# Gates as one stacked fp32r product, and a norm's factors made a row by two fp32r products, in a two-layer decoder trunk

## The chip, the cores and the metric

The kernel runs on 1 core of one Trainium2 chip. The metric is the device time of one execution in microseconds (us). The engines are PE (matrix products; PEld is its loading of weights), DVE (vector), ACT (scalar, activation functions), POOL and SP (here it issues the transfers). L12 is line 12 of the kernel before.

## The reference

The input is 256 tokens of width 2048, with 256 memory tokens. Layer 0 mixes with gated linear attention (GLA, 4 heads), layer 1 with forgetting attention; both cross-attend into the memory, and each is followed by a gated MLP of width 5632 with a short convolution. Everything is fp32. What the change touches is the norm, used throughout, and the gates of GLA:

```python
def rmsnorm(x, g):
    xf = x.astype(jnp.float32)
    y = xf * lax.rsqrt(jnp.mean(xf * xf, axis=-1, keepdims=True) + EPS)
    return (y * g.astype(jnp.float32)).astype(x.dtype)
...
    z = h @ w_in
    q, k, v, glr, og, mq = split_cols(
        z, [GLA_QK_WIDTH, GLA_QK_WIDTH, GLA_V_WIDTH, GLA_GATE_RANK, GLA_V_WIDTH, MEM_WIDTH])
    g = jax.nn.log_sigmoid((glr @ w_gate_up + b_gate).astype(jnp.float32)) / GLA_GATE_TAU
```

`glr` has 16 columns, `w_gate_up` is 16 x 1024.

## The kernel before, in words

**Products.** A PE product takes fp32 operands, or fp32r ones, which hold fewer bits. The large projections keep fp32 accuracy by three fp32r products: each weight tile `raw` (loaded by SP, L189) is rounded to `whi` by ACT (L190), and the rest, `wlo = raw - whi`, comes from DVE (L199). Activations are split in the same way (`split`, L283) into the pairs in `bufA` and `bufB`. The product of the two rests is left out. `raw` has four buffers, `whi` and `wlo` three each.

**Two kinds of projection.** `proj_fm` (L202) gives outputs with features on the partitions: for each of 16 row blocks and two column blocks, L224 multiplies `whi` by both parts side by side (512 columns) and L225 `wlo` by the high part (256 columns); L227 closes. `proj_tm` (L237) gives outputs with tokens on the partitions (L261, L262, L263). Together they are nearly all of PE's work.

**Norms.** The factor of a norm is one number per token, and it is applied to a projection's result. `Norm.col` (L328) makes it as a column, tokens on the partitions, by a sum and three Newton steps on DVE (L323 to L326). `Norm.row` (L339) makes of it a row that is the same on all partitions: DVE builds a diagonal matrix of the factors, `dg`, by two products of the identity with a column (L345), PE multiplies a matrix of ones by it in fp32 (L347), and ACT copies the result (L350). This happens nine times: for the memory's norm, for the mixer's norm of layer 0, for each of four GLA heads, for the two MLP norms, and for the norm that keys, values and layer 1's mixer share. `dg` takes a buffer of the tag "sq", of which there are two, and which the squares of the norms use too (L302, L363).

**Gates.** The first value projection of GLA has the 16 gate columns beside it. `turned` (L267) takes them: ACT writes them, scaled, into `narrow`, a tile of zeros (L273), PE transposes it (L278), and ACT copies the result to `glr` (L490): 16 used rows of 128. For each head, `gates` (L505) loads its 128x256 weights `wg` (L509; two buffers; rows beyond 16 are zeros) and makes two fp32 products of 128x256 (L513), whose results go through Abs, Exp and Ln on ACT (L516 to L518) and a scan on DVE (L522). `turned` serves the forget gates of layer 1 as well (L658).

**Order.** A scheduler orders the instructions of each engine when the program is built, from the dependences, from estimated times, and from a priority that draws the weight loads and splits ahead (`tc.high_priority`, L194). Engines then run their lists in order. SP's list holds nearly all loads.

Of the kernel before, what the change touches and what calls it, by code (L numbers as in the profile page):

```python
# [12 lines left out]
F32 = mybir.dt.float32  # L13
F32R = mybir.dt.float32r
I32 = mybir.dt.int32
AF = mybir.ActivationFunctionType
ALU = mybir.AluOpType
PSUM = bass.MemoryType.PSUM

P = 128  # L20
T = 256
# [4 lines left out]
GLA_H, DK, DV = 4, 256, 384  # L26
FOX_H, HD = 12, 128
MEM_H = 4
RANK = 16
# [107 lines left out]
def _trunk(ctx: ExitStack, tc: tile.TileContext, xt, xtok, memt, wp, wgu, gns, gfin, cnv, par, msk, out):  # L137
    nc = tc.nc
    where, _ = _layout()
    V, S, TE = nc.vector, nc.scalar, nc.tensor  # L140

    const = ctx.enter_context(tc.tile_pool(name="const", bufs=1))
    wpool = ctx.enter_context(tc.tile_pool(name="wpool", bufs=4))
    sm = ctx.enter_context(tc.tile_pool(name="small", bufs=2))
# [9 lines left out]
    ident = mask[:, M_ID : M_ID + P]  # L154
    ones = mask[:, M_ONE : M_ONE + P]
# [3 lines left out]
    def gain(name, i):  # L159
        c = C_GAIN[name] + i  # L160
        return gains[:, c : c + 1]

    eps = const.tile([P, 1], F32, name="eps")
    nc.gpsimd.memset(eps, EPS)

# [10 lines left out]
    def work(tag, bufs=1):  # L176
        return pwork.tile([P, 512], F32, name="ps_" + tag, tag=tag, bufs=bufs)
# [86 lines left out]
                if u == len(units) - 1:  # L264
                    evac(b, a)

    def turned(pool, bank, width, col):  # L267

        t = pool.tile([P, T], F32, name="narrow", tag="tmp", bufs=5)
        nc.gpsimd.memset(t, 0.0)  # L270

        def take(b, a):
            S.activation(t[:, b * P : b * P + width], a, AF.Copy, scale=col[:, b : b + 1])  # L273

        def turn():
            for b in range(2):
                bs = slice(b * P, (b + 1) * P)
                TE.transpose(bank[:, bs], t[:, bs], ident)  # L278
            return bank[:, :T]

        return take, turn
# [11 lines left out]
    class Norm:  # L293
# [45 lines left out]
        def row(self):  # L339

            if self.r is None:
                y = self.col()
                dg = sm.tile([P, T], F32, name="dg", tag="sq", bufs=2)
                for b in range(2):
                    V.tensor_scalar(dg[:, b * P : (b + 1) * P], ident, y[:, b : b + 1], None, ALU.mult)  # L345
                pr = work("t")
                TE.matmul(pr[:, :T], ones, dg, start=True, stop=True)  # L347
                self.r = sm.tile([P, T], F32, name="row", tag="rowx" if self.tag == "x" else "row",
                                 bufs=2 if self.tag == "x" else 1)
                S.activation(self.r, pr[:, :T], AF.Copy)  # L350
            return self.r
# [51 lines left out]
    nx = StreamNorm()  # L403
# [65 lines left out]
    def gla(nx):  # L469
        h, mix = bufB, bufA  # L470
        with tc.tile_pool(name="gla", bufs=1) as gp:
# [3 lines left out]
                nc.gpsimd.memset(t, 0.0)  # L475
            on = {}

            glr = gp.tile([P, T], F32, name="glr")

            def values(hd):  # L480
                return gp.tile([P, 2, DV], F32, name="gv", tag="gv", bufs=2)

            v0 = values(0)
            take, turn = turned(gp, work("t"), RANK, nx.col())

            def first_values(b, a):
                S.activation(v0[:, b, :], a[:, :DV], AF.Copy, scale=nx.col()[:, b : b + 1])
# [17 lines left out]
            def gates(hd):  # L505

                bc = gp.tile([P, 2, T], F32, name="bc", tag="bc", bufs=2)
                wg = gp.tile([P, DK], F32, name="wg", tag="wg", bufs=2)
                nc.sync.dma_start(wg, wgu[hd])  # L509
                for c in range(2):  # L510
                    f = 2 * hd + c
                    ps = work("s", 2)
                    TE.matmul(ps[:, :T], wg[:, c * P : (c + 1) * P], glr, start=True, stop=True)  # L513
                    bias = part[:, C_BG + f : C_BG + f + 1]
                    e = gp.tile([P, T], F32, name="ge", tag="tmp", bufs=5)
                    S.activation(e, ps[:, :T], AF.Abs, bias=bias)  # L516
                    S.activation(e, e, AF.Exp, scale=-1.0)
                    S.activation(e, e, AF.Ln, bias=1.0)  # L518
                    mz = gp.tile([P, T], F32, name="gm", tag="tmp", bufs=5)
                    V.tensor_scalar(mz, ps[:, :T], bias, 0.0, ALU.add, ALU.min)  # L520
                    V.tensor_tensor(mz, mz, e, ALU.subtract)
                    V.tensor_tensor_scan(bc[:, c, :], scanmask, mz, 0.0, ALU.mult, ALU.add)  # L522
                return bc
# [100 lines left out]
            for hd in range(GLA_H):  # L624
                bc = gates(hd)
                q = gp.tile([P, 2, T], F32, name="gq", tag="gq", bufs=2)
                k = gp.tile([P, 2, T], F32, name="gk", tag="gk", bufs=2)
                v = values(hd) if hd else v0
                proj_fm(("gq", hd), h, lambda c, a: V.scalar_tensor_tensor(
                    q[:, c, :], whole(a), DK ** -0.5, nx.row(), ALU.mult, ALU.mult))  # L630
                proj_fm(("gk", hd), h, lambda c, a: V.tensor_tensor(k[:, c, :], whole(a), nx.row(), ALU.mult))
                if hd == GLA_H - 1:
                    for j in range(OG_EARLY):
                        take_og(j)
                if hd:
                    proj_tm(("gv", hd), h, lambda b, a: S.activation(
                        v[:, b, :], a, AF.Copy, scale=nx.col()[:, b : b + 1]))
                core(hd, q, k, v, bc)
# [4 lines left out]
    def fox(nx, vt):  # L643
        hk, hq, mix = bufB, bufA, bufB
        stash = vt.rearrange("p b (i t) -> p (b i) t", t=T)
        with (
# [9 lines left out]
            cs = fp.tile([P, T], F32, name="fc")  # L656
            cc = fp.tile([P, 2, FOX_H], F32, name="fcc")
            take, turn = turned(fp, work("s", 2), FOX_H, nx.col())  # L658

            def forget():  # L660
# [120 lines left out]
    def preparing(name, dst, also=None):  # L781
# [18 lines left out]
        return n, then  # L800

    gla(nx)
    n, then = preparing("ffn0", bufB)
    add_out(("wo", 0), bufA, then)
# [18 lines left out]
    with tc.tile_pool(name="store", bufs=1) as op:  # L823
        gf = op.tile([P, D], F32, name="gf")
        nc.sync.dma_start(gf, gfin.to_broadcast([P, D]))
        y = op.tile([P, 2, 512], F32, name="y")
# [93 lines left out]
```

## Time and profile before

| | |
|---|---|
| median of 3 runs | 2309.28 us (2309.21 to 2309.69) |
| the profiled execution: its own time | 2308.97 us |
| its span, first to last instruction | 2307.2 us |
| granted PE clock | 0.999 |
| busy PE, DVE, ACT | 2289.1, 1605.6, 1251.5 us |
| weight splits L199 (DVE) | 972.6 us in 809 |
| weight roundings L190 (ACT) | 843.2 us in 809 |
| PE records of L347 (row) and L513 (gates) | 18 and 16 |
| mean transfer rate | 186 GB/s |

Each group of the profile names the line, the engine, the operation, the tiles (out<-in) and the shapes, then the busy time, the mean duration of one, and the engine's idle time just before, with what ended it. Durations of PE records overlap, since products follow each other in its pipe; what a product costs is read from the distance between starts. A product of fp32 operands leaves two records of products and two of weight loads, one of fp32r operands a single one of each.

### The profile page before, as it was taken

What the parts mean: (1) busy time and instruction counts of PE and PEld (TensorE: products, weight loads), DVE (VectorE), ACT (ScalarE), POOL (GpSimd) and SP (SyncE); (2) the same over time, 40 slices, a digit from 0 to 9 for tenths busy, and PEclk for the clock granted to TensorE, in tenths of its full rate; (3) what the DMA queues carried; (4) which work ended last, traced back from release to release, by engine and by line L of the source; (5) the groups of instructions that cost most, each with busy time, mean ns of one, the idle gap of its engine ahead of it and who ended that gap; (6) DMA issues with size and microseconds to landing.
All of it is one profiled execution on the core that took longest, in us unless ns stands there. A gap on an engine that the chain in (4) does not pass through costs nothing.

```text
span 2307.2 us, 32826 instructions
## 1 busy us (share of the span) xinstructions
PE 2289.1 (99%) x12256; PEld 1986.0 (86%) x12256; DVE 1605.6 (70%) x2595; ACT 1251.5 (54%) x1954; POOL 3.0 (0%) x19
## 2 busy tenths in 40 slices
PE   8999999999999999999999999999999999999998
PEld 7889998888888888888888998888888888888886
DVE  7567877577774777557767557657776577756775
ACT  6555555455553555445565455556554455534554
POOL 0000000000000000000000000000000000000000
PEclk9999999999999999999999999999999999999999
DMA  8655455655555555655555564565556555565554
GB/s 305 204 161 158 147 163 166 192 185 185 190 192 191 192 186 189 192 192 191 187 186 184 172 207 151 163 198 183 191 186 192 194 187 191 186 196 190 186 191 155
DMA packets 124744, 430.27 MB, mean 186 GB/s; under 512 B 14108, under 2 KB 18600, under 8 KB 124456
## 3 DMA queue, kind: packets, MB, share of 16 engines
q1 hardware_dynamic: 124296, 427.65, 57.6%
q8 instruction: 96, 1.57, 0.3%
q10 hardware_dynamic: 288, 0.52, 0.1%
q14 instruction: 64, 0.52, 0.1%
HBM read 426.01 MB, written 2.11 MB: 186 GB/s over the span
## 4 chain that ended last, share of the span: by engine, by line
PE 98%; DMA 0%; ACT 0%; DVE 0%; issue 0%; SPq 0%; DVEq 0%; ACTq 0%
PE acc L224 37%; PE acc L225 20%; PE acc L262 12%; PE acc L263 12%; PE acc L261 12%; PE acc L227 2%; PE ps_s L588 1%; PE ps_s L794 0%; PE ps_t L379 0%; PE ps_s L386 0%; PE ps_o L397 0%; DMA mt<-memt 0%; PE ps_s L708 0%; PE ps_o L602 0%; PE ps_o L724 0%; PE ps_s L557 0%
## 5 line engine op out<-in xcount | busy, mean ns | idle before, releaser
L199 DVE TENSOR_TENSOR wlo<-raw,whi 128x1024 fp32r<-128x1024 f32 (+4 forms) x809 | 972.6, 1203 | 554.1 <-ACT whi L190 541.4
L190 ACT ACTIVATE whi<-raw 128x1024 fp32r<-128x1024 f32 (+4 forms) x809 | 843.2, 1043 | 779.6 <-PE acc L263 366.6
L224 PE MATMUL acc<-B,whi 128*128 128x512 f32 x1980 | 683.4, 395 | 0.0
L224 PE MATMUL acc<-A,whi 128*128 128x512 f32 x1680 | 580.6, 396 | 7.4 <-ACT whi L190 7.4
L225 PE MATMUL acc<-B,wlo 128*128 128x256 f32 x2112 | 551.4, 281 | 0.0
L225 PE MATMUL acc<-A,wlo 128*128 128x256 f32 x1792 | 464.5, 281 | 0.5 <-DVE wlo L199 0.5
L224 PEld LDWEIGHTS acc<-B,whi 128*128 128x128 f32 x1980 | 361.0, 188 | 68.3
L225 PEld LDWEIGHTS acc<-B,wlo 128*128 128x128 f32 x2112 | 397.6, 188 | 20.8
L224 PEld LDWEIGHTS acc<-A,whi 128*128 128x128 f32 x1680 | 305.8, 188 | 64.0 <-ACT whi L190 7.7
L225 PEld LDWEIGHTS acc<-A,wlo 128*128 128x128 f32 x1792 | 338.1, 189 | 21.0 <-DVE wlo L199 1.2
L262 PE MATMUL acc<-wlo,B 128*128 128x512 f32 (+3 forms) x736 | 275.4, 374 | 1.2 <-DVE wlo L199 1.2
L263 PE MATMUL acc<-whi,B 128*128 128x512 f32 (+3 forms) x736 | 273.7, 372 | 0.0
L261 PE MATMUL acc<-whi,B 128*128 128x512 f32 (+3 forms) x736 | 247.8, 372 | 0.0
L262 PE MATMUL acc<-wlo,A 128*128 128x512 f32 x544 | 212.4, 390 | 0.0
L263 PE MATMUL acc<-whi,A 128*128 128x512 f32 x544 | 212.0, 390 | 0.0
L261 PE MATMUL acc<-whi,A 128*128 128x512 f32 x544 | 192.8, 391 | 0.0
L232 ACT ACTIVATE part<-acc 128x256 f32<-128x256 f32 x240 | 90.1, 375 | 165.4 <-PE acc L227 165.4
L262 PEld LDWEIGHTS acc<-wlo,B 128*128 128x128 f32 x736 | 138.2, 188 | 20.6 <-DVE wlo L199 1.5
L263 PEld LDWEIGHTS acc<-whi,B 128*128 128x128 f32 x736 | 138.2, 188 | 18.9
L261 PEld LDWEIGHTS acc<-whi,B 128*128 128x128 f32 x736 | 137.4, 188 | 18.7
L234 DVE TENSOR_TENSOR wholes<-acc,part 128x256 f32<-128x256 f32 x240 | 101.0, 421 | 67.4 <-ACT part L232 67.3
L263 PEld LDWEIGHTS acc<-whi,A 128*128 128x128 f32 x544 | 102.1, 188 | 21.2
(196 smaller groups left out, 1576.1 us busy)
## 6 DMA issues: line engine op xcount, KB each, us to landing
raw<-wp SPq DMA_DIRECT2D x743, 512.0 KB, 3.4
raw<-wp SPq DMA_DIRECT2D x32, 384.0 KB, 3.1
raw<-wp SPq DMA_DIRECT2D x24, 388.0 KB, 3.1
raw<-wp SPq DMA_DIRECT2D x8, 400.0 KB, 3.1
xf<-xt SPq DMA_DIRECT2D x16, 128.0 KB, 4.7
x<-xtok SPq DMA_DIRECT2D x4, 512.0 KB, 7.1
mt<-memt SPq DMA_DIRECT2D x3, 512.0 KB, 7.8
cb<-cdram SPq DMA_DIRECT2D x12, 128.0 KB, 3.4
```

The lines of the kernel that those rows point to most:

```text
L190: casts.append(S.activation(hi[:, s], raw[:, s], AF.Copy))
L199: V.tensor_tensor(lo[:, s], raw[:, s], hi[:, s].bitcast(F32), ALU.subtract)
L224: TE.matmul(a, hi[:, s], both, start=done == 0, stop=False)
L225: TE.matmul(a[:, :T], lo[:, s], both[:, 0, :], start=False, stop=False)
L227: TE.matmul(a, hi[:, s], both, start=False, stop=True)
L232: S.activation(t, a[:, T:], AF.Copy)
L234: V.tensor_tensor(r, a[:, :T], t, ALU.add)
L261: TE.matmul(a, xk[:, 0, xs], hi[:, s], start=u == 0 and j == 0, stop=False)
L262: TE.matmul(a, xk[:, 0, xs], lo[:, s], start=False, stop=False)
L263: TE.matmul(a, xk[:, 1, xs], hi[:, s], start=False, stop=last)
L588: TE.matmul(ps[:, b * NVER : (b + 1) * NVER], kt[:, c, b * P : (b + 1) * P], dd[:, 2 * c + b, :], start=c == 0, stop=c == 1)
```

## The change

Both fp32 products named above become fp32r products.

The row: the factors `y` are split into a rounded part and the rest, each a column pair in fp32r. For each part DVE makes a diagonal tile of 128x256 by one product of the identity with the broadcast column, and PE multiplies a tile of ones in fp32r (filled once by POOL) by it; the two products add up in one accumulator.

The gates: the three partial products of a split multiplication (high by high, high by rest, rest by high) are laid along the rows that were zeros. `narrow` now holds the rounded gate columns at 0 and at 32 and their rest at 64; the weights hold the same 16 rows three times, and rows 32 to 63 are replaced by the rest of the rounding, so that one fp32r product sums all three. `wg` is loaded as `raw`, rounded by ACT and its middle rows are subtracted by DVE; `wgraw` and `wg` have one buffer each. The forget gates of layer 1 keep the old way.

```diff
+    onesr = const.tile([P, P], F32R, name="onesr")
+    nc.gpsimd.memset(onesr.bitcast(F32), 1.0)
...
-    def turned(pool, bank, width, col):
+    def turned(pool, bank, width, col, parts=False):
...
         def take(b, a):
-            S.activation(t[:, b * P : b * P + width], a, AF.Copy, scale=col[:, b : b + 1])
+            o = [t[:, b * P + i : b * P + i + width] for i in (0, 32, 64)]
+            if not parts:
+                S.activation(o[0], a, AF.Copy, scale=col[:, b : b + 1])
+                return
+            for i in range(2):
+                S.activation(o[i].bitcast(F32R), a, AF.Copy, scale=col[:, b : b + 1])
+            V.scalar_tensor_tensor(o[2], a, col[:, b : b + 1], o[0], ALU.mult, ALU.subtract)
...
                 y = self.col()
-                dg = sm.tile([P, T], F32, name="dg", tag="sq", bufs=2)
-                for b in range(2):
-                    V.tensor_scalar(dg[:, b * P : (b + 1) * P], ident, y[:, b : b + 1], None, ALU.mult)
+                y2 = [sm.tile([P, 2, 1], F32R, name=f"y{i}", tag=f"y{i}") for i in range(2)]
+                V.tensor_copy(y2[0], y.unsqueeze(2))
+                V.tensor_tensor(y2[1], y.unsqueeze(2), y2[0].bitcast(F32), ALU.subtract)
                 pr = work("t")
-                TE.matmul(pr[:, :T], ones, dg, start=True, stop=True)
+                for i, yi in enumerate(y2):
+                    dg = sm.tile([P, 2, P], F32R, name="dg", tag="sq", bufs=2)
+                    V.tensor_tensor(dg, ident.unsqueeze(1).to_broadcast([P, 2, P]),
+                                    yi.bitcast(F32).to_broadcast([P, 2, P]), ALU.mult)
+                    TE.matmul(pr[:, :T], onesr, dg, start=i == 0, stop=i == 1)
...
-            glr = gp.tile([P, T], F32, name="glr")
+            glr = gp.tile([P, T], F32R, name="glr")
...
-            take, turn = turned(gp, work("t"), RANK, nx.col())
+            take, turn = turned(gp, work("t"), RANK, nx.col(), True)
...
-                wg = gp.tile([P, DK], F32, name="wg", tag="wg", bufs=2)
-                nc.sync.dma_start(wg, wgu[hd])
+                raw = gp.tile([P, DK], F32, name="wgraw", tag="wgraw")
+                nc.sync.dma_start(raw, wgu[hd])
+                wg = gp.tile([P, DK], F32R, name="wg", tag="wg")
+                S.activation(wg, raw, AF.Copy)
+                V.tensor_tensor(wg[32:64], raw[32:64], wg[32:64].bitcast(F32), ALU.subtract)
...
-    wgu[:RANK] = a["gla_w_gate_up"][0]
+    for i in (0, 32, 64):
+        wgu[i : i + RANK] = a["gla_w_gate_up"][0]
```

## The prediction

> **What bounds the kernel now.** I read the page first: the busy shares, then the chain that ended last.
>
> ```profile
> PE 2289.1 (99%) x12256; PEld 1986.0 (86%) x12256; DVE 1605.6 (70%) x2595; ACT 1251.5 (54%) x1954; POOL 3.0 (0%) x19
> ...
> PE 98%; DMA 0%; ACT 0%; DVE 0%; issue 0%; SPq 0%; DVEq 0%; ACTq 0%
> ```
>
> The matrix engine (PE) is busy for 99% of the span, and 98% of the last chain is its own products, one after the other. A busy share alone could hide gaps between products, so the view of waits comes next, for PE alone (who waits for whom: us in total, times, longest):
>
> ```profile
> PE acc L224 <- ACT whi L190: 7.4, 1, 7.4
> PE acc L262 <- DVE wlo L199: 1.2, 1, 1.2
> PE acc L225 <- DVE wlo L199: 0.5, 1, 0.5
> ```
>
> PE waits three times: for the first data, once at the start, and once at 1321 us. Nothing else stops it. The granted clock is 0.999. So the kernel lasts as long as its list of products, and a shorter product shortens it one for one, as long as no wait appears.
>
> **What the change takes from PE.** The groups by form show the two products that are replaced, and an fp32r product of the same 256 columns (the last pair of numbers before the bar's idle: busy us, mean ns):
>
> ```profile
> L225 PE MATMUL acc<-B,wlo 128*128 128x256 f32 x2112 | 551.4, 281 | 0.0
> ...
> L347 PE MATMUL ps_t<-dg,mask 128*128 128x256 f32 x18 | 5.3, 378 | 0.0
> L513 PE MATMUL ps_s<-glr,wg 128*128 128x256 f32 x16 | 4.8, 379 | 0.0
> ```
>
> L347 is the norm's row and L513 the gates. An fp32 product leaves two records, so 18 and 16 records are nine rows and eight gate products. The mean durations are no price: products overlap in the pipe, so I take the distance between starts. The timeline of PE around the row of the last GLA head:
>
> ```profile
> 396.56 0.39 PE L261 MATMUL acc<-whi,A 128*128 128x512 f32 x1
> 396.79 0.40 PE L262 MATMUL acc<-wlo,A 128*128 128x512 f32 x1
> 397.02 0.59 PE L347 MATMUL ps_t<-dg,mask 128*128 128x256 f32 x2
> 397.27 0.58 PE L263 MATMUL acc<-whi,A 128*128 128x512 f32 x1
> 397.68 0.63 PE L261 MATMUL acc<-whi,A 128*128 128x512 f32 x2
> ```
>
> From L262 (396.79) to L261 (397.68) are 0.89 us. The same stretch without a row, L262 and L263, takes two steps of 0.23 us (396.56 to 396.79 is one). The row costs 0.89 - 0.46 = 0.43 us. A gate, in the timeline at head 0:
>
> ```profile
> 160.12 0.28 PE L225 MATMUL acc<-B,wlo 128*128 128x256 f32 x1
> ...
> 160.23 0.59 PE L513 MATMUL ps_s<-glr,wg 128*128 128x256 f32 x2
> ...
> 160.47 0.58 PE L224 MATMUL acc<-B,whi 128*128 128x512 f32 x1
> ...
> 160.89 1.02 PE L397 MATMUL ps_o<-pts,mv 128*128 128x256 f32 x4
> ```
>
> From L225 to L397 are 0.77 us, and L225 plus L224 take 0.35 (0.117 + 0.232, the median distances of starts behind these lines in the trace): the gate costs 0.42 to 0.43. So 17 products x 0.43 = **7.31 us** go.
>
> **What it adds on PE.** Nine rows become 18 fp32r products of 128x256, eight gates become eight: 26. In the trace an L225 is followed by an L224 after 117 ns (median of 3,140), and by another L225 after 114 (median of 499). I take 117: 26 x 0.117 = **3.04 us**. The bounds: 0.112 (the lowest tenth) and 0.124 (the highest), so 2.9 to 3.2. Nothing gives a gain below that, since 256 columns are streamed in every case.
>
> One rule of the Trainium skill speaks against this step. Its page "TensorE: Matmul & The Clock Gate", section "The mechanism" of the part on packing, says that a weight load overlaps a running product only when the two use different row groups; here all use the whole array. The same page puts a load of 128 columns at about 107 ns, so 26 loads in the open would be an estimated 2.8 us, and the sum would nearly vanish. The trace disagrees: 499 pairs of L225, each with its own full load (188 ns in the PEld rows), follow at 114 ns, which leaves no room for a load in the open.
>
> **What it adds elsewhere.** Per row, DVE's two diagonal halves become a copy, a difference, and two products of 128x256. The nearest rows:
>
> ```profile
> L572 DVE TENSOR_TENSOR gdd<-bc 128x256 f32<-128x256 f32 x12 | 5.0, 418 | 0.0
> ...
> L345 DVE TENSOR_SCALAR dg<-mask,ny 128x128 f32<-128x128 f32 x18 | 4.3, 283 | 0.2
> L324 DVE TENSOR_TENSOR nt<-nt,nv 128x2 f32<-128x2 f32 x27 | 4.3, 158 | 0.6
> ```
>
> Two L345 take 0.48 us from start to end. The new chain takes two small steps of 0.2 us (L323 to L326 start that far apart) and 2 x 0.42: about 1.24, 0.76 more per row, 6.8 us in nine. The bounds of one wide step are 0.28 (L345, half as wide) and 0.55 (L572 at 384 columns). For the gates come four DVE differences of 32x256 (at most 0.42 each, 1.7 us), four ACT conversions of 128x256 (0.38 by the row's copy at L350, 1.5 us), two more narrow ACT evictions (0.26 by L273 at 12 columns) and two narrow DVE ones (0.16 to 0.35). That is about 9 us of DVE and 2 us of ACT. What hides them: ACT's weight conversions L190 sit idle for 366.6 and 217.0 us until PE (L263, L224) frees a buffer, and DVE's L199 waits 541.4 us for ACT. Both run as far ahead as their three buffers let them. Without that cover each microsecond counts in full, but only inside the buffer's depth, some 2.8 us of PE work per weight tile.
>
> The added waits: PE waits for two diagonals instead of one. How early was the one? At the first channel mixer's row:
>
> ```profile
> 494.53 0.48 DVE L345 TENSOR_SCALAR dg<-mask,ny 128x128 f32<-128x128 f32 x2
> 495.25 1.23 DVE L199 TENSOR_TENSOR wlo<-raw,whi 128x1024 fp32r<-128x1024 f32 x1 [0.24 <-ACT whi L190]
> ...
> 498.83 0.59 PE L347 MATMUL ps_t<-dg,mask 128*128 128x256 f32 x2
> ```
>
> The diagonal is done at 495.01, 3.8 us before PE comes to it; over the nine rows the least is 3.4 us (the head at 327.01). As built, the changed program puts one weight split L199 between the factors' split and the diagonals here and in two more rows, and between the diagonals of two heads. Here: 494.93 after the two small steps, L199 to 496.5, diagonals to 497.3. The built program also sets the products later, some 1.7 us of PE work here, so about 3 us stay. Behind a PE product that waits stand all weight products; behind a DVE diagonal stands the next L199, which PE needs units later. Both diagonals now hold the two "sq" buffers, so ACT's squares wait for the second product; no square is due within several us, except at the memory norm, where they wait for x (landing near 55.9) anyway.
>
> The loads of `wg` stay four of 128 KB (4.2 us to landing), through one buffer. The second now stands behind three more weight loads on SP and waits for the first one's DVE split. SP's weight loads behind it wait for DVE's splits too, and gates are first needed at 160 us, the first load goes out at 39. I put this at nothing. The ones tile is a POOL memset near 0.7 us, against PE's first product at 7.37.
>
> The order moves much else within GLA, but the costly change of shape there, the 64-column products L552, comes in seven runs before and after. The stall at 1321 us follows the forget gates (two ACT table loads, a transfer out and three back on SP); none of it is touched.
>
> **Sum.** 7.31 - 3.04 = 4.27 us less. The profiled execution took 2308.97 us around its span of 2307.2, so 2304.7; it lies 0.3 below the median of the runs shown. Against that median, 2309.28 - 4.27 = **2305.0 us**, 0.185% faster. A measurement of this kernel tells about 0.2%, that is 4.62 us (2304.66), from no change: the forecast falls just short of it.
>
> **Rivals.**
> - Part of it is eaten: one or several rows or weight splits in GLA come late, 0.5 to 4 us of waits. For it: DVE is 79% busy from 120 to 290 us (133.99 of 170) and gets most of the new work. Against: PE waited for nothing there. 2305.6 to 2309. Chance 0.16.
> - Slower: DVE's chain to the second diagonal misses PE at the eight rows whose cover is only a few us (the ninth has 52). If each is late by one weight split, 1.23 us, that is 9.8: 2314.8. From 0.53 us per row it is slower than before. For it: the chain grows by 0.76 us and at places by a split. Against: the 3 us counted above. Chance 0.06, 0.04 of it beyond 0.2%.
> - More: the stall at 1321 us (1.2) or changes of shape in GLA shrink too. 2303.4 to 2304.4, chance 0.09.
> - It doesn't do what it says: 26 products at 0.43 are 11.2 us, 3.9 more than before, 2313.2. Against: L225's steps. Chance 0.02.
> - The added weight loads stand open: 26 x 0.188 by the PEld rows, 4.9 us, 2309.9. This is what the skill's rule above would give. Chance 0.01, by the 114 ns.
>
> **The numbers.** The forecast, 2304.4 to 2305.6, has 0.66, a quarter of it (0.17) under 2304.66. Faster: 0.17 + 0.09 = 0.26. Slower: 0.04. Within: 0.70. The range reaches from 2303.6 to 2307.5: it leaves out the slow cases, the upper half of the eaten one and the edge of the gain.
>
> **What would show it.** PE's groups: the rows as 18 records of about 280 ns instead of 378, the gates as eight; steps of 0.11 to 0.12 us behind them. PE's waits: still three. If a fourth appears, on the row's line or on L199 between 35 and 400 us, one of the first two rivals holds; if the list has three and the time differs by over 1 us, my price of a product is wrong.

## The result, and the profile after

| | before | changed kernel |
|---|---|---|
| median, 19 runs each on one chip | 2309.23 us | 2305.37 us |
| lowest to highest | 2308.3 to 2311.47 | 2304.29 to 2306.77 |
| profiled execution: own time / span | 2308.97 / 2307.2 | 2305.43 / 2303.7 |
| granted PE clock | 0.999 | 0.999 |

The changed kernel takes 0.9983 of the time before, with a 95% interval of 0.9977 to 0.9989: 3.86 us less, 2.5 to 5.3 by the interval. The forecast was 4.27 us less and 2305.0 us; the time lies 0.4 us above it, inside the range, and on the side of the line where it was put (less than 0.2% faster). 0.4 us is less than the interval can tell. But two readings beside the forecast turned out wrong, and the traces show a loss of some tenths of a microsecond that was not on the list.

The page of the changed kernel first: busy shares, and the chain that ended last.

```profile
PE 2286.3 (99%) x12248; PEld 1983.3 (86%) x12248; DVE 1611.1 (70%) x2619; ACT 1253.2 (54%) x1960; POOL 3.1 (0%) x20
...
PE 98%; DMA 0%; ACT 0%; DVE 0%; issue 0%; SPq 0%; DVEq 0%; ACTq 0%
```

PE's records fall by 8 (16 of the gates become 8, 18 of the rows stay 18), DVE grows by 5.5 us and ACT by 1.7. The chain is still 98% PE. In the changed kernel's code the weight rounding is L192, the split L201, the products of `proj_fm` L226, L227, L229, those of `proj_tm` L263 to L265, the row's product L361 and the gate's L530. Who makes PE wait (us in total, times, longest):

```profile
PE acc L226 <- ACT whi L192: 6.7, 2, 6.2
PE acc L264 <- DVE wlo L201: 1.1, 1, 1.1
PE acc L227 <- DVE wlo L201: 0.5, 1, 0.5
```

The same three lines as before. The first now counts twice: a wait of 0.5 us has come in at 12.2 us, while the first transfers land. None stands at a row or a gate. The two new groups, by form (busy us, mean ns):

```profile
L361 PE MATMUL ps_t<-dg,onesr 128*128 128x256 f32 x18 | 5.1, 294 | 0.0
...
L530 PE MATMUL ps_s<-glr,wg 128*128 128x256 f32 x8 | 2.7, 342 | 0.0
```

The counts are those forecast. The mean durations are not the price; the distance between starts is. The row of the last GLA head, in PE's timeline (start, duration, in us):

```profile
393.81 0.40 PE L263 MATMUL acc<-whi,A 128*128 128x512 f32 x1
394.04 0.28 PE L361 MATMUL ps_t<-dg,onesr 128*128 128x256 f32 x1
394.16 0.39 PE L264 MATMUL acc<-wlo,A 128*128 128x512 f32 x1
394.39 0.28 PE L361 MATMUL ps_t<-dg,onesr 128*128 128x256 f32 x1
394.51 0.40 PE L265 MATMUL acc<-whi,A 128*128 128x512 f32 x1
```

From 393.81 to 394.51 there are 0.70 us for two weight products of 0.23 and two row products: 0.12 each, 0.24 for the row where it was 0.43. On DVE, the chain that now ends in two wide products, at the first channel mixer's row:

```profile
491.77 0.16 DVE L355 TENSOR_TENSOR y<-ny,y 128x2 fp32r<-128x2 f32 x1
492.29 1.23 DVE L201 TENSOR_TENSOR wlo<-raw,whi 128x1024 fp32r<-128x1024 f32 x1 [0.36 <-ACT whi L192]
493.43 0.76 DVE L359 TENSOR_TENSOR dg<-mask,y 128x256 fp32r<-128x256 f32 x2
```

The weight split stands between the factors' split and the diagonals, as the built order said. The diagonals end at 494.19; PE comes to the first row product at 497.39. 3.2 us of cover stay, against "about 3" in the prediction.

**Where the time went.** Following the same product through both traces, the changed kernel is level at 55 us, about 2.9 us ahead at 398, 3.5 at 1238 and 3.5 at the end. Most of it comes in GLA, where the eight gates and five of the nine rows are.

### The profile page after: what moved, and what is told of

Read it like the earlier page. It is cut to its first block, busy times and chain, and to the rows that moved or that the text cites. A ratio compares the mean times of both kernels' runs of the same rounds, so it can differ in the third digit from the quotient of the medians.

```text
span 2303.7 us, 32841 instructions
## 1 busy us (share of the span) xinstructions
PE 2286.3 (99%) x12248; PEld 1983.3 (86%) x12248; DVE 1611.1 (70%) x2619; ACT 1253.2 (54%) x1960; POOL 3.1 (0%) x20
## 4 chain that ended last, share of the span: by engine, by line
PE 98%; DMA 0%; ACT 0%; DVE 0%; issue 0%; SPq 0%; DVEq 0%; ACTq 0%
PE acc L226 37%; PE acc L227 20%; PE acc L264 12%; PE acc L265 12%; PE acc L263 12%; PE acc L229 2%; PE ps_s L605 1%; PE ps_s L811 0%; PE ps_t L393 0%; PE ps_s L400 0%; PE ps_o L411 0%; DMA mt<-memt 0%; PE ps_s L725 0%; PE ps_o L741 0%; PE ps_o L619 0%; PE ps_s L574 0%
## 5 line engine op out<-in xcount | busy, mean ns | idle before, releaser
L201 DVE TENSOR_TENSOR wlo<-raw,whi 128x1024 fp32r<-128x1024 f32 (+4 forms) x809 | 972.9, 1203 | 546.6 <-ACT whi L192 535.3
L192 ACT ACTIVATE whi<-raw 128x1024 fp32r<-128x1024 f32 (+4 forms) x809 | 843.2, 1043 | 772.8 <-PE acc L265 372.8
L226 PE MATMUL acc<-B,whi 128*128 128x512 f32 x1980 | 682.9, 395 | 0.0
L226 PE MATMUL acc<-A,whi 128*128 128x512 f32 x1680 | 581.5, 397 | 6.7 <-ACT whi L192 6.7
L227 PE MATMUL acc<-B,wlo 128*128 128x256 f32 x2112 | 550.6, 281 | 0.0
L227 PE MATMUL acc<-A,wlo 128*128 128x256 f32 x1792 | 464.7, 281 | 0.5 <-DVE wlo L201 0.5
L226 PEld LDWEIGHTS acc<-B,whi 128*128 128x128 f32 x1980 | 360.8, 188 | 68.1
L227 PEld LDWEIGHTS acc<-B,wlo 128*128 128x128 f32 x2112 | 397.6, 188 | 20.9
L226 PEld LDWEIGHTS acc<-A,whi 128*128 128x128 f32 x1680 | 306.0, 188 | 63.7 <-ACT whi L192 7.4
L227 PEld LDWEIGHTS acc<-A,wlo 128*128 128x128 f32 x1792 | 338.5, 189 | 21.1 <-DVE wlo L201 1.4
L265 PE MATMUL acc<-whi,B 128*128 128x512 f32 (+3 forms) x736 | 273.6, 372 | 0.0
L263 PE MATMUL acc<-whi,B 128*128 128x512 f32 (+3 forms) x736 | 247.0, 372 | 0.0
L265 PE MATMUL acc<-whi,A 128*128 128x512 f32 x544 | 211.8, 389 | 0.0
L263 PE MATMUL acc<-whi,A 128*128 128x512 f32 x544 | 192.4, 390 | 0.0
L265 PEld LDWEIGHTS acc<-whi,B 128*128 128x128 f32 x736 | 138.3, 188 | 18.8
L263 PEld LDWEIGHTS acc<-whi,B 128*128 128x128 f32 x736 | 137.4, 188 | 18.5
L236 DVE TENSOR_TENSOR wholes<-acc,part 128x256 f32<-128x256 f32 x240 | 101.1, 421 | 63.7 <-ACT part L234 63.6
L265 PEld LDWEIGHTS acc<-whi,A 128*128 128x128 f32 x544 | 102.1, 188 | 21.2
```

The costliest lines, as they stand in the source:

```text
L192: casts.append(S.activation(hi[:, s], raw[:, s], AF.Copy))
L201: V.tensor_tensor(lo[:, s], raw[:, s], hi[:, s].bitcast(F32), ALU.subtract)
L226: TE.matmul(a, hi[:, s], both, start=done == 0, stop=False)
L227: TE.matmul(a[:, :T], lo[:, s], both[:, 0, :], start=False, stop=False)
L236: V.tensor_tensor(r, a[:, :T], t, ALU.add)
L263: TE.matmul(a, xk[:, 0, xs], hi[:, s], start=u == 0 and j == 0, stop=False)
```

## The experiments

The theory: the gain is the sum of shorter products on PE alone (17 x 0.43 less, 26 x 0.117 more), and DVE's longer chain costs nothing. The rivals: the products' prices differ from mine, or the longer chain costs something at some rows, or the new transfers and buffers do. Medians of one kernel, taken at different times, differ by some tenths (2308.5 to 2309.4 for the kernel before), so I use a second measure beside it, from the profiled execution: the time from PE's 90th product (counted from 0) to its last. It leaves out the first 26 us, in which the first transfers land: that 90th product starts anywhere from 24.8 to 28.3 us in the executions here. For two executions of the changed kernel this measure is 2268.25 and 2268.59 us, before it is 2271.99. An execution of the kernel before with one unused tile added (`pad`, below) has 2272.45, so less than half a microsecond means little by it.

### The two parts alone

`rows_only` is the changed kernel with the gates as before, `gates_only` the one with the rows as before.

> Only the norms' rows are changed; the gates stay one fp32 product each. Theory (time is PE's list of products): nine rows x (0.43 - 2 x 0.117) = 1.8 us less than before, PE still waits three times, and each row shows a step down of about 0.2 us in PE's progress. Rival (late diagonals eat it): between 1.8 us less and some us more, with a new wait of PE on a row's line. Rival (the gain is luck of the new order in GLA): not near 1.8, and the five rows outside GLA show no step.

> Only the gates are changed; the rows stay one fp32 product. Theory: 8 x (0.43 - 0.117) = 2.5 us less than before, all of it between 155 and 300 us of the span; with rows_only it adds up to the whole change. Rival (order): the two halves do not add up, since each is scheduled anew. Rival (weight rounding and splits of the gates on ACT and DVE cost time): less than 2 us.

| | median of 11 | ratio to before, 95% | change of the time from the 90th product | counted in the sum |
|---|---|---|---|---|
| rows_only | 2307.57 us | 0.9995 (0.9986 to 1.0004) | -1.66 us | 9 x (0.43 - 0.234) = 1.76 |
| gates_only | 2305.98 us | 0.9989 (0.998 to 0.9998) | -2.45 us | 8 x (0.43 - 0.117) = 2.50 |

The kernel before, measured beside them, had 2308.9 us, so the medians are 1.3 and 2.9 us less. By the medians alone the rows' gain could be nothing; by the trace both parts bring what was counted, within 0.1 us, which is closer than this measure can promise. Together they make 4.1 us, but the changed kernel shows 3.4 to 3.7. A stricter count starts at 120 us and leaves out the one wait behind that, of 1.1 us near 1318 us: by it both executions of the changed kernel are 3.50 us ahead of before, `pad` 0.00, the two parts 1.42 and 2.46. So some tenths are lost when both are there.

### The price of each product, nine times over

`row32_x9` is the kernel before with each row's fp32 product made nine times (72 more), `row32r_x9` the changed kernel with each of the two fp32r products made nine times (144 more). Both divide by nine when the row is copied.

```diff
-                    TE.matmul(pr[:, :T], onesr, dg, start=i == 0, stop=i == 1)
+                    for n in range(9):
+                        TE.matmul(pr[:, :T], onesr, dg, start=i + n == 0, stop=i + n == 9)
...
-                S.activation(self.r, pr[:, :T], AF.Copy)
+                S.activation(self.r, pr[:, :T], AF.Copy, scale=1 / 9)
```

> The kernel before with each row's fp32 product made nine times into one accumulator, and the copy scaled by 1/9: 9 x 8 = 72 more fp32 products of 128x256. Theory: the price by starts, 0.43 us: 31 us more than before (0.427 by columns alone gives 30.7). Rival (the price is the mean duration of the records, two of 0.378): 54 us more. Rival (some of a row's product lay in idle time of PE): well over 31.

> The changed kernel with each of a row's two fp32r products made nine times, the copy scaled by 1/9: 18 x 8 = 144 more fp32r products of 128x256, each with a full weight load. Theory: 0.114 to 0.117 us each, 16.4 to 16.8 us more than the changed kernel, 12.5 to 13 more than before. Rival (weight loads stand open, 0.188 us each): 43 us more than the changed kernel, 39 more than before. Rival (128 us of columns only, no cost of switching, 0.107): 15.4, so 11.5 more than before.

`row32_x9` has a median of 2340.16 us against 2308.9: 31.26 us for 72 products, **0.434 us** each (ratio 1.0137, 1.0121 to 1.0152). `row32r_x9` has 2321.24: 12.3 us over before, which with the 3.86 us that the change saves makes 16.2 us for 144, **0.113 us** each (1.0054, 1.004 to 1.0067; by the time from the 90th product, 0.115 to 0.117). The prices taken were 0.43 and 0.117. With the measured ones the sum would be 17 x 0.434 - 26 x 0.113 = 4.4 us. The prices are not where the 0.4 us went.

The rule that a weight load overlaps a running product only in other row groups (the Trainium skill, "TensorE: Matmul & The Clock Gate", "The mechanism") is not borne out here: these 144 products each have a record of a load of the whole array, 188 ns long, and cost 113 ns in all. The same section also lets loads into a background weight buffer go ahead of running products, and that is the part that the runs fit.

### How long may DVE's chain become?

The change makes the chain 0.76 us longer per row. These three kernels make it longer still, by Newton steps that change nothing in a factor that is already found: four small operations each, 0.8 us a step.

```diff
-                self.newton(self.y, v, 3)
+                self.newton(self.y, v, 9)
```

> The changed kernel with nine Newton steps instead of three in each norm's factors: 6 x 4 more DVE instructions of 0.2 us, 4.8 us longer from a norm's sum to its diagonals, nine times; the result's value stays. Theory (DVE's chain is covered, and the scheduler places the products later): same as the changed kernel within 0.3 us, no new wait of PE. Rival (the cover counted is 3 us and then PE waits): at the eight rows with a few us of cover (4.8 - 3) each, 14 us more than the changed kernel.

> The changed kernel with 21 Newton steps: the chain is 14.4 us longer. Theory: cover ends where a row is needed to empty the accumulators: two projections of about 11 us can run on before that, so at the rows of the two channel mixers and of the shared norm some us may appear, in GLA's four heads nothing: 0 to 6 us more than the changed kernel. Rival (cover of 3 us at eight rows): 8 x 11.4 = 91 us more.

`newton9` (4.8 us longer) has 2305.8 us, 0.9986 of before (0.9976 to 0.9995), and no wait of PE at L361: it costs a few tenths at most (by the stricter count 3.13 us ahead of before instead of 3.50). `newton21` (14.4 us longer) has 2362.63, 57 us over the changed kernel. Neither number on record covers it: the theory, which had the scheduler move the row back as far as needed, and the rival, which had every row pay in full, are both out. PE waits for the diagonal at four rows only, 7.6, 5.0, 6.6 and 5.0 us: the last GLA head, the first channel mixer, the shared norm and the second channel mixer. At the other five PE does not wait for the diagonal. `newton15` (9.6 us) was made to see where it begins:

> The changed kernel with 15 Newton steps: the chain from a norm's sum to its diagonals is 9.6 us longer. By the run with 21 steps (14.4 us longer; PE waited 7.6, 5.0, 6.6 and 5.0 us for a diagonal, at the last GLA head, the two channel mixers and the shared norm), the cover there is about 7 to 9 us: waits of 2.8, 0.2, 1.8 and 0.2 us, 5 us or more in all, with what stands behind them perhaps 10 more than the changed kernel. Rival (cover of 3 us at eight rows): 50 us more.

It has 2326.33 us (1.0078, 1.0063 to 1.0094), 21 us over the changed kernel, where some 10 were expected and 50 by the rival. PE's waits, two of the list's six lines:

```profile
PE acc L226 <- DVE wholes L236: 9.6, 4, 3.3
...
PE ps_t L361 <- DVE dg L359: 0.3, 1, 0.3
```

Read at the row's own line, all seems well: 0.3 us. The cost stands one step further on. The accumulators are emptied by DVE (L236 into `wholes`), whose buffers are held until the row arrives; with the row late, PE has no free accumulator and its next weight product waits. PE's timeline at the first channel mixer (the bracket is PE's wait and who ended it):

```profile
522.61 0.39 PE L361 MATMUL ps_t<-dg,onesr 128*128 128x256 f32 x2
526.27 0.77 PE L226 MATMUL acc<-B,whi 128*128 128x512 f32 x1 [3.27 <-DVE wholes L236]
```

The waits in this list are 13 us more than in the changed kernel's, and the time is 21 us more. The windows view of PE (length, busy, granted clock, share of the DMA engines, GB/s) tells of most of the rest:

```profile
526.30:529.00 2.70, 2.70 (x9) 0.50 0.46 176
529.00:532.00 3.00, 3.00 (x18) 0.97 0.00 0
```

After a wait of 3.27 us PE runs for 2.7 us at half the clock: 9 products where the next 3 us hold 18. The trace has three stretches of half the clock that the changed kernel has not, 3.4 us each: this one, one behind a wait of 2.5 us at 1266 us, and one behind three waits of 0.5 to 1.2 us between 410 and 416 us. Together they cost 5.1 of the 8 us that the waits leave open; the rest was not traced. So waits of a few microseconds can cost more than themselves, but they need not. At the second channel mixer's row PE waits 3.27 us too, until 1616.39, and the clock stays full:

```profile
1616.40:1619.40 3.00, 3.00 (x17) 1.00 0.43 161
```

The Trainium skill ("TensorE: Matmul & The Clock Gate", Part 1, "What's actually happening") says that the clock is halved after an idle window of about 3.4 us and full again after a busy one, and that these windows run free of the kernel. The 0.50 and the 3.4 us agree; the waits that led to it here are shorter than such a window.

So the cover is larger than the prediction had it ("about 3 us stay"): the limit is past 4.8 us of added chain. By the waits it is near 14.4 - 7.6 = 6.8 at the last GLA head in `newton21`, and near 9.6 - 3.3 = 6.3 at the first channel mixer in `newton15`. The reason: the 3 us are those of the orders before and after, but when the chain grows, the scheduler puts the row's product later, as far as the accumulators allow. At the first channel mixer 2,324 products of the projections stand ahead of it in the changed kernel, 2,378 with nine steps, and 2,432 both with 15 and with 21. The rival "slower" by a late diagonal took its length as its price, at eight rows. A diagonal that is late costs more than that, but at fewer rows, and the 0.76 us that the change adds to the chain are far from making one late.

### The wait at 1321 us: SP's queue or DVE's order?

The prediction had this wait follow the forget gates ("two ACT table loads, a transfer out and three back on SP"). If SP's queue is the cause, other queues should shrink it:

```diff
-            nc.sync.dma_start(cdram, cs[:FOX_H, :])
+            nc.gpsimd.dma_start(cdram, cs[:FOX_H, :])
...
-                nc.sync.dma_start(pb, cdram[hd : hd + 1, :].to_broadcast([P, T]))
+                nc.gpsimd.dma_start(pb, cdram[hd : hd + 1, :].to_broadcast([P, T]))
```

> The changed kernel with the forget gates' transfer out and the twelve transfers back issued by POOL instead of SP, so that SP's weight loads no longer stand behind them. Theory: the wait of PE at 1317 us (1.1 us) goes, 1.1 to 1.3 us less than the changed kernel. Rival (the two ACT table loads ahead of it hold the weight roundings, and the wait stays): same as the changed kernel. Rival (POOL's issue is slower): DVE's L720 waits for cb, and PE with it: more.

> The changed kernel once more, for a second profile beside the others. If the 0.4 us between the sum (4.27) and the medians (3.86) is noise of an execution, PE's progress against before differs in the places where it lost time in the first profile (0.2 us by 12 us, 0.3 us between 122 and 180 us, 0.2 us between 1430 and 1485 us); if it comes from the order as built, the places are the same.

`again` is the changed kernel once more, measured beside it: 2305.09 us, 0.9982 (0.9973 to 0.9991). `pool_queue` has 2308.44, 0.9996 (0.9987 to 1.0004), and the wait grew from 1.1 to 2.2 us: SP's queue was not it. The transfers back are slower this way: 0.54 us of POOL for one issue where SP takes 0.33, and 4.0 us to landing instead of 3.3. DVE waits longer for the first one, as the last rival had it:

```profile
1319.13 0.35 DVE L720 SCALAR_TENSOR_TENSOR dm<-cb,fcc,mask 128x128 f32<-128x128 f32 x1 [4.28 <-DMA cb<-cdram]
```

That is about 1 of the 3 us by which this median lies above the changed kernel's; the rest is open. In the changed kernel's timeline, the stretch before the wait:

```profile
1317.10 0.35 DVE L720 SCALAR_TENSOR_TENSOR dm<-cb,fcc,mask 128x128 f32<-128x128 f32 x1 [3.03 <-DMA cb<-cdram]
...
1317.37 0.48 DVE L722 SCALAR_TENSOR_TENSOR dm<-cb,fcc,mask 128x256 f32<-128x256 f32 x1
...
1317.76 0.96 DVE L201 TENSOR_TENSOR wlo<-raw,whi 128x776 fp32r<-128x776 f32 x1
...
1318.78 0.44 PE L264 MATMUL acc<-wlo,B 128*128 128x388 f32 x1 [1.14 <-DVE wlo L201]
```

DVE stands 3.03 us at L720, which builds the decay mask of the first head of the forgetting attention, until its transfer lands. L201 stands behind it in DVE's list, though its own input had been ready since 1316.06, and PE waits for L201. In the kernel before, DVE waits 3.06 us at the same operation (L703). The list of waits names L201 and hides L720. If that is so, it is enough to put the mask's two operations behind the weight split (`splits` collects the L201 instructions as they are made):

```diff
-                V.scalar_tensor_tensor(dm[:, :P], pb[:, :P], cc[:, 0, hd : hd + 1], foxmask[:, P:],
-                                       ALU.subtract, ALU.add)
-                V.scalar_tensor_tensor(dm[:, P:], pb[:, :T], cc[:, 1, hd : hd + 1], foxmask, ALU.subtract, ALU.add)
+                with tc.issue_after(splits[-1].ins):
+                    V.scalar_tensor_tensor(dm[:, :P], pb[:, :P], cc[:, 0, hd : hd + 1], foxmask[:, P:],
+                                           ALU.subtract, ALU.add)
+                    V.scalar_tensor_tensor(dm[:, P:], pb[:, :T], cc[:, 1, hd : hd + 1], foxmask, ALU.subtract, ALU.add)
```

> The changed kernel with the forget masks' two DVE instructions per head queued behind the last weight split of their own query projection, so that DVE no longer stands before the transfer of c (3.0 us at 1317 us) with weight splits behind it. Theory (that DVE wait, not SP's queue, makes PE's stall): the stall of 1.1 to 1.3 us goes, 1.1 to 1.3 us less than the changed kernel. Rival (SP's weight loads behind the transfers make the stall): it stays, same as the changed kernel. Rival (the masks are late for the heads): PE waits in the attention, more.

The median is 2303.85 us, 0.9979 (0.997 to 0.9988). PE's waits are down to two lines:

```profile
PE acc L226 <- ACT whi L192: 5.7, 1, 5.7
PE acc L227 <- DVE wlo L201: 0.4, 1, 0.4
```

The wait is gone. SP still issues all the transfers, the first three at the same place in its list; two later ones, and some instructions behind the wait, changed places. From the 90th product on it is 1.1 us less than in the changed kernel (2267.14 against 2268.25), and 1.3 to 1.4 us are gained at the place itself. The medians alone don't show it: against the kernel before measured beside each, this one is 4.6 us less, the changed kernel 3.9 and 4.3.

### The missing tenths

Comparing the starts of products that have the same neighbours in both orders, some steps from a 512-column weight product to the 256-column one behind it take 239 to 250 ns where most others take 230 to 237. How often they do so repeats from one execution of a program to the next. Behind 55 us the two executions of the changed kernel differ in nothing but the wait at 1318 us (1.1 and 1.3 us), so the loss belongs to the program as built.

| steps of 239 to 250 ns | 120 to 182 us | 182 to 400 | 400 to 1240 | 1380 to 1490 | 1570 to the end |
|---|---|---|---|---|---|
| before | 8 | 28 | 105 | 8 | 101 |
| gates_only | 10 | 41 | 105 | 8 | 101 |
| rows_only | 18 | 39 | 98 | 29 | 94 |
| changed kernel, two executions | 22, 22 | 35, 36 | 98, 98 | 28, 28 | 94, 94 |
| dm_late | 22 | 35 | 98 | 29 | 94 |
| pad | 8 | 28 | 105 | 8 | 101 |
| y_wide | 16 | 20 | 104 | 6 | 100 |

Two of the rises come with the new rows: at 120 to 182 us, and at 1380 to 1490 us, where the order of PE's products is the same as before. (Between 182 and 400 us `gates_only` has the most without them, for a reason that was not looked for, and in the two long stretches the new rows go with seven fewer.) That suggests something outside PE's order: where tiles lie in memory. `pad` is the kernel before with an unused constant tile of 512 bytes per partition, as large as the new tile of ones, so that all behind it lies 512 bytes later.

```diff
+    pad = const.tile([P, P], F32, name="pad")
+    nc.gpsimd.memset(pad, 1.0)
```

> The kernel before with one more constant tile of 128x128 that nothing reads, in the place of the changed kernel's ones; every engine's order stays. Theory (some products of weights take 11 ns longer where the tiles lie otherwise in the memory): the steps from a product of 512 columns to the next that take 239 to 250 ns rise from 8 to about 22 between 120 and 182 us and from 7 to about 27 between 1380 and 1490 us, as in every kernel with the new rows, and 0.3 us are lost. Rival (the new instructions of the rows cause it): 8 and 7 as before.

No count moved, as the rival had it: 2308.66 us in its one run. But the change adds a second thing: the two small tiles of the split factors, two buffers each. `y_wide` is `dm_late` with these tiles 64 bytes per partition wide instead of 8, of which the first 8 are used. Every engine's list of instructions is that of `dm_late`.

```diff
-                y2 = [sm.tile([P, 2, 1], F32R, name=f"y{i}", tag=f"y{i}") for i in range(2)]
+                y2 = [sm.tile([P, 16, 1], F32R, name=f"y{i}", tag=f"y{i}")[:, :2] for i in range(2)]
```

> dm_late once more, with the two little tiles of the factors' parts taking 64 bytes per partition each instead of 8 (only their first two columns are used), so that everything behind them lies 224 bytes later; every engine's list of instructions is the same. In the changed kernel the step from a 512-column weight product to the next is 239 to 250 ns instead of 232 or less in some stretches: 22 and 29 times in the windows 120 to 182 and 1380 to 1490 us of dm_late, 8 and 7 times in the kernel before and in the kernel with an unused tile of 512 bytes. Theory (addresses): the 8-byte tiles shift all tiles behind them by an odd amount, and the longer steps come from where operands lie; then the counts fall to about 8 and 7 and the time falls by 0.2 to 0.4 us, about 2303.5. Rival (not the addresses: they belong to the order of the new products or to something else in the program): the counts stay within three of 22 and 29, and the time stays within 0.2 us of dm_late's, 2303.85, as far as a median tells that.

One number in this has to be corrected: as built, tiles are placed in steps of 32 bytes, so an 8-byte tile takes 32, and what lies behind the four buffers moves by 4 x 32 = 128 bytes, not 224. Against the kernel before, tiles behind both additions lie 512 bytes later in `pad`, 512 + 128 = 640 in the changed kernel, and 768 in `y_wide`.

The count at 1380 to 1490 us falls from 29 to 6, that at 182 to 400 from 35 to 20, that at 120 to 182 only to 16. The same three products in `dm_late`:

```profile
1415.33 0.40 PE L226 MATMUL acc<-A,whi 128*128 128x512 f32 x1
1415.58 0.28 PE L227 MATMUL acc<-A,wlo 128*128 128x256 f32 x1
1415.69 0.40 PE L226 MATMUL acc<-A,whi 128*128 128x512 f32 x1
```

and in `y_wide`:

```profile
1415.90 0.39 PE L226 MATMUL acc<-A,whi 128*128 128x512 f32 x1
1416.13 0.27 PE L227 MATMUL acc<-A,wlo 128*128 128x256 f32 x1
1416.25 0.40 PE L226 MATMUL acc<-A,whi 128*128 128x512 f32 x1
```

The first step is 241 ns there and 231 here. Against `dm_late`, `y_wide` gains 0.4 us between 55 and 400 us and 0.46 us between 1380 and 1490, and loses 0.1 to 0.2 us near 500 us and again behind 1490: 0.6 us less behind 55 us, 0.8 from the 90th product on. That is more than the 0.2 to 0.4 expected, since the counts catch only part of it. The median is 2302.77 us (0.9972, 0.9961 to 0.9983), 1.1 us under `dm_late`'s; their single runs overlap, and so do the intervals of the two ratios. It is the fastest version of all: 6.3 us under the kernel before measured beside it.

What follows: the addresses of tiles change PE's steps, with nothing else changed. They are not the addresses of what these products read. The pools are allocated in the order `const` (with bufA and bufB), `wpool` (`raw`, `whi`, `wlo`) and `small`, which has the new little tiles; as built, the operands of the products shown lie at the same place in `dm_late` and `y_wide`. What moved are tiles behind them, which mostly ACT and DVE use, such as `wholes` and those of the attention. How that reaches PE's steps is open. The shifts by 512 and 768 bytes have the few long steps and the one by 640 the many, which would fit a rule in multiples of 256; three shifts don't show one. Which tile it is, and which addresses are good, wasn't tried and stays open.

## Why the prediction was right, step by step

- **What bounds the kernel.** Right. The shorter products shortened it one for one, and products made nine times lengthened it at the same prices.
- **The prices.** Right: 0.43 forecast and 0.434 measured for an fp32 product; 0.117 and 0.113 to 0.117 for an fp32r one. The rivals "it doesn't do what it says" (26 at 0.43) and "the added weight loads stand open" (26 x 0.188) fall with the second. One remark beside them was wrong: the estimated 2.8 us of open loads would have left 1.5 of the 4.27 us, so the sum would not "nearly vanish".
- **What it adds elsewhere.** Right in what matters. The wide diagonals took 418 ns each (0.42 forecast), the factors' two steps start 0.2 us apart, and ACT's and DVE's new work is hidden: PE's waits show none of it, at any row, gate or load of `wg`. The totals were set too high: DVE grew by 5.5 us where 9 were counted, ACT by 1.7 where 2 were.
- **The cover of the diagonal.** Right at the place that was counted (3.2 us at the first channel mixer against about 3), wrong as a limit: 4.8 us more cost a few tenths at most, 9.6 us more cost 21.
- **The wait at 1321 us.** That the change leaves it alone was right (1.2 before, 1.1 after). What makes it was not seen: not the weight loads behind the transfers on SP's queue, but a weight split standing behind a DVE operation that waits for the first of these transfers. It is worth 1.1 to 1.4 us.
- **The sum.** 4.27 us forecast, 3.86 measured, which the interval (2.5 to 5.3) can't tell apart; by the trace from the 90th product on, 3.4 to 3.7. A term that no step of the prediction looked at is the change of addresses. By the stricter count (from 120 us on, without the wait) eight rows and eight gates are left, and the sum for them is 16 x 0.43 - 24 x 0.117 = 4.1, or 4.2 by the measured prices. The changed kernel shows 3.5 of it and `dm_late` 3.4; `y_wide`, with other addresses, shows 4.0. So the addresses account for most of what was missing, and the last tenths are open.
- **The forecast and its line.** "Within 0.2%" had 0.70 and came out, at 0.17%. That is in part luck: the forecast lay 0.35 us from the line, the interval is 2.8 us wide, and the loss by addresses moved the time away from the line. "Part of it is eaten" had the sign of the 0.4 us right but by another mechanism: no row or split came late.

## What to carry to other kernels

Where one engine is busy for 99% and 98% of the last chain, count that engine's work by distances between starts, and the sum holds to some tenths of a microsecond. For each wait that is left, look in the waiting engine's releaser for what stands ahead of it in its in-order list: the operation named in the list of waits may itself only be queued behind another wait. When a difference of tenths can't be found in the instructions, compare addresses: a small new tile moves everything that is allocated behind it.

## What the runs showed of the hardware that was not expected

- The same list of products runs 0.6 to 0.8 us faster or slower in 2270 us, in part by steps of 241 ns instead of 230, when tiles that those products don't read are moved by 128 bytes against the others; moving all but the first few tiles by 512 bytes changed no count.
- After waits of 0.5 to 3.3 us PE's granted clock was 0.50 for 3.4 us at three places of `newton15`, and stayed full behind another wait of 3.3 us; 13 us of waits cost 21 us there, and the longer ones of `newton21` led to 57 us (its mean clock is 0.990, that of `newton15` 0.996).
- The first 26 us vary by up to 3.5 us between executions, by when the first transfers land. That is as large as the whole gain of this change, and is why its size had to be read in traces.
